# A layer of latent attention and gated MLP: one turn of three PSUM banks, later key stores, a float32 last block

## The chip, the core and the metric

The kernel runs on one core of a Trainium2 chip. The metric is the device time of one execution in microseconds (us), as a median of several runs. The core has five engines that work through queues of their own: TensorE (PE, matrix products; its loads of the stationary operand are listed as PEld), VectorE (DVE), ScalarE (ACT), GpSimd (POOL) and SyncE (SP), which here only issues transfers. PSUM, where matrix products arrive, has eight banks of 128 x 512 float32.

## What is computed

The layer takes `x`, 2048 tokens of 1024 features, projects it, mixes it in two branches, and projects back.

```python
y = rms_norm(h, norm_in_g)
proj = jnp.einsum("bsd,de->bse", y, w_in)
q_lat, kv_lat, k_rope, gate_mla, u, v, gate_gmlp = jnp.split(proj, bounds, axis=-1)
o_mla = mla_branch(q_lat, kv_lat, k_rope, q_norm_g, w_uq, kv_norm_g, w_ukv)
o_gmlp = gmlp_branch(jax.nn.gelu(u, approximate=False), jax.nn.gelu(v, approximate=False),
                     gmlp_ln_g, gmlp_ln_b, w_spatial, b_spatial)
o_mla = rms_norm(o_mla, out_norm_mla_g) * jax.nn.silu(gate_mla)
o_gmlp = rms_norm(o_gmlp, out_norm_gmlp_g) * jax.nn.silu(gate_gmlp)
h = h + jnp.einsum("bse,ed->bsd", jnp.concatenate([o_mla, o_gmlp], axis=-1), w_out)
return rms_norm(h, final_norm_g)
```

The attention branch has 8 heads of 64 + 32 (rotary) key features and 128 value features. The rotary key is one for all heads. The mask is causal by chunks of 64: a query sees all keys of its chunk and of the chunks before.

## The kernel before

Tokens are tiled by 512 (four tiles `t`), in two halves `hf` of two tiles. Nearly every product is made from three passes: each operand is split into a high part of a shorter float32 type (`fp32r`, names ending in `h`) and the rest (`l`), and high x high, low x high and high x low are added up in PSUM. Each half runs through the stages values of the gate (`v`), query latents, queries, key and value latents (`stage_kv`), keys and values (`stage_ukv`), gates (`gm`) and the gated MLP (`stage_ug`, products `u` and `g` with weights loaded as `ws_ug` and split into `wh_ug` on ScalarE and `wl_ug` on VectorE, and `sp`, a plain float32 product with the spatial matrix). `stage_kv` turns the rotary keys with a selecting matrix `sel` (L518), splits them on ScalarE and VectorE (L521, L82) and writes each part to `kh_d` or `kl_d` for all eight heads, 512 KB a store (L524). `stage_ukv` stores keys (L464) and values (`vh_d`, `vl_d`, L559, L560).

Attention runs over 32 units, 8 heads `h` by 4 query tiles `j` of 512 (heads 0 and 7 with `j` from 3 down). A unit has `nk` = 4j + 4 blocks of 128 keys, the last four of them on the diagonal. Block `kb` makes scores `ss` by three matmuls (L832 to L834), one exponential, the split into `ph` and `pl`, and three matmuls into `po` (L872 to L874). Odd blocks take their exponentials on ScalarE and their subtraction on VectorE (L82), even ones subtract on GpSimd (L866); row sums build up in `accv` and `accg` (L854, L870, L881). Diagonal block i uses columns from 128 i on, but at most from 256: the fourth (kb = nk - 1) has 256 columns, half of them filled with zero (L842, L843). Then the sums are turned and reduced (`pzs`, L92, L93), their reciprocals spread (`pzr`, L99), and the output scaled (L888).

Ahead of it, `row_maxima` makes a maximum for each query row: products `px` (L168), each read by one or two reductions into `mx` (L173, L175), and at the end of a unit `mz`, `pzm` (L145) and the last rows of `qh` (L146). Between the blocks stand products of the MLP's output projection (`pg`), handed out by `side()`, as long as there are any. After attention come the rows of the attention output: `mla_rows` (`sq`, `zm`, row sums `s`, the product `pr` with a column of ones, `zmh`, `zml`) and the projection `pm`.

PSUM during attention: `px` and `pzm` turn in two banks (`ps_x`), `pzs`, `pzr` and `pr` use one (`ps_z`), `ss` two, `po` one, `pe` two. A scheduler with a timeline of its own orders the instructions of each engine, so that small edits move others; each engine then works strictly in its order. The order excerpts below are from it.

## Time and profile before

| | |
|---|---|
| median of three timed runs | 1889.8 us (1889.35 to 1889.97) |
| profiled execution | 1891.02 us, of it the span 1889.2 |
| TensorE busy | 1857.7 us, 98% of the span |
| VectorE, ScalarE, GpSimd busy | 1111.1, 788.1, 582.8 us |
| granted clock of TensorE, mean | 0.994 |

Times in the rows are counted from the start of the span. Attention runs from about 1022 to 1702 us, the last projection from there to the end. Busy time says how long an engine had an instruction at hand; a printed matmul overlaps the next, so what a matmul costs is read from one start to the next. A granted clock of 1 is 2.4 GHz, 0.5 is 1.2.

### The profile page before, as it was taken

How to read it: one execution, taken by the hardware profiler on the slowest of the kernel's cores; microseconds unless marked ns; L12 is line 12 of the kernel's file. 1: busy time of each engine (PE TensorE's matmuls, PEld its weight loads, DVE VectorE, ACT ScalarE, POOL GpSimd, SP SyncE). 2: the span in 40 equal slices, each digit the busy share in tenths (PEclk: the TensorE clock that was granted, in tenths of full speed). 3: DMA queues.
4: the chain of work that ended last, by engine and by line, in shares of the span. 5: the costliest groups of instructions: out<-in, count | busy, mean ns of one | idle time of the engine just before them, and what ended most of it. 6: DMA issues, size and time to landing. Idle time of an engine off the chain costs nothing.

```text
span 1889.2 us, 24722 instructions
## 1 busy us (share of the span) xinstructions
PE 1857.7 (98%) x8638; PEld 1536.8 (81%) x8638; DVE 1111.1 (59%) x1866; ACT 788.1 (42%) x1440; POOL 582.8 (31%) x644
## 2 busy tenths in 40 slices
PE   8999999999999999999999999999999999999998
PEld 6888877888888887888887788888888888778886
DVE  7235454665622463557766677676677776665553
ACT  6232233522422332333213655555555555573332
POOL 5000100122100010012224645464545455564332
PEclk9999999999999999999998999999999999999999
DMA  7225387955432253986427653343425242445653
GB/s 253 91 74 190 104 249 255 306 158 156 156 105 73 97 195 90 290 273 190 135 91 226 181 156 101 106 125 110 142 68 166 76 132 83 141 162 182 201 190 107
DMA packets 251173, 292.28 MB, mean 155 GB/s; under 512 B 17188, under 2 KB 166692, under 8 KB 250792
## 3 DMA queue, kind: packets, MB, share of 16 engines
q1 hardware_dynamic: 250904, 290.69, 48.7%
q8 instruction: 69, 1.13, 0.3%
q14 instruction: 56, 0.46, 0.1%
q10 hardware_dynamic: 144, 0.00, 0.0%
HBM read 181.58 MB, written 111.15 MB: 155 GB/s over the span
## 4 chain that ended last, share of the span: by engine, by line
PE 90%; DMA 3%; DVE 3%; issue 2%; ACT 1%; POOL 1%; DVEq 0%; SPq 0%; POOLq 0%; ACTq 0%
PE px L168 3%; PE ss L832 3%; PE ss L833 3%; PE ss L834 3%; PE po L874 3%; PE po L872 3%; PE po L873 3%; PE pm L911 3%; PE pg L910 3%; PE pg L911 3%; PE pm L912 3%; PE pm L910 3%; PE u L107 3%; PE pg L912 3%; PE u L109 3%; PE g L109 3%
## 5 line engine op out<-in xcount | busy, mean ns | idle before, releaser
L175 DVE TENSOR_REDUCE mx<-px 128x1 f32<-128x512 f32 (+2 forms) x320 | 180.3, 580 | 34.0 <-PE px L168 31.6
L870 POOL TENSOR_TENSOR accg<-accg,p 128x512 f32<-128x512 f32 (+1 forms) x104 | 118.0, 1134 | 189.0 <-ACT p L864 138.4
L82 DVE TENSOR_TENSOR pl<-ss,ph 128x512 fp32r<-128x512 f32 (+2 forms) x160 | 93.2, 583 | 138.6 <-ACT ss L848 124.9
L866 POOL TENSOR_TENSOR pl<-p,ph 128x512 fp32r<-128x512 f32 (+1 forms) x128 | 150.9, 1179 | 40.2 <-ACT ph L865 19.3
L639 POOL TENSOR_TENSOR z<-gu,ggt 128x512 f32<-128x512 f32 x32 | 42.0, 1312 | 365.4 <-DVE ggt L627 245.0
L847 ACT ACTIVATE ph<-ss 128x512 fp32r<-128x512 f32 (+2 forms) x160 | 82.1, 513 | 130.7 <-PE ss L834 112.2
L874 PE MATMUL po<-pl,vh 128*128 128x512 f32 (+1 forms) x320 | 120.4, 376 | 5.3 <-POOL pl L866 3.7
L832 PE MATMUL ss<-qh,kh 100*128 100x512 f32 (+1 forms) x320 | 120.1, 375 | 1.4 <-ACT p L864 0.7
L872 PE MATMUL po<-ph,vh 128*128 128x512 f32 (+1 forms) x320 | 119.6, 374 | 0.2 <-ACT ph L847 0.2
L833 PE MATMUL ss<-ql,kh 96*128 96x512 f32 (+1 forms) x320 | 118.9, 372 | 0.0
L834 PE MATMUL ss<-qh,kl 96*128 96x512 f32 (+1 forms) x320 | 118.5, 370 | 0.0
L168 PE MATMUL px<-kh,qh 96*128 96x512 f32 (+2 forms) x320 | 111.2, 386 | 6.0 <-DVE mx L175 4.7
L873 PE MATMUL po<-ph,vl 128*128 128x512 f32 (+1 forms) x320 | 117.0, 365 | 0.0
L910 PE MATMUL pg<-woh,zgh 128*128 128x512 f32 x256 | 101.8, 398 | 0.0
L107 PE MATMUL u<-yh,wh_ug 128*128 128x512 f32 x256 | 101.7, 397 | 0.0
L911 PE MATMUL pm<-wol,zmh 128*128 128x512 f32 x256 | 101.6, 397 | 0.0
L107 PE MATMUL gm<-yh,wh_gm 128*128 128x512 f32 x256 | 101.0, 395 | 0.4 <-DVE kf L440 0.4
L911 PE MATMUL pg<-wol,zgh 128*128 128x512 f32 x256 | 101.3, 396 | 0.0
L912 PE MATMUL pg<-woh,zgl 128*128 128x512 f32 x256 | 100.7, 393 | 0.0
L108 PE MATMUL gm<-yl,wh_gm 128*128 128x512 f32 x256 | 100.4, 392 | 0.0
L910 PE MATMUL pm<-woh,zmh 128*128 128x512 f32 x256 | 100.4, 392 | 0.0
L109 PE MATMUL gm<-yh,wl_gm 128*128 128x512 f32 x256 | 100.4, 392 | 0.0
(567 smaller groups left out, 4938.1 us busy)
## 6 DMA issues: line engine op xcount, KB each, us to landing
ws_ug<-in_w_in SPq DMA_DIRECT2D x32, 512.0 KB, 5.0
xt<-in_x_t SPq DMA_DIRECT2D x16, 512.0 KB, 5.9
gv_d<-gv SPq DMA_DIRECT2D x32, 256.0 KB, 2.0
ws_gm<-in_w_in SPq DMA_DIRECT2D x16, 512.0 KB, 4.5
gt_d<-gth SPq DMA_DIRECT2D x32, 256.0 KB, 2.7
lgv<-gv_d SPq DMA_DIRECT2D x32, 256.0 KB, 3.5
wos<-in_w_out SPq DMA_DIRECT2D x16, 512.0 KB, 3.8
z_d<-z SPq DMA_DIRECT2D x32, 256.0 KB, 3.1
```

Of the source, the lines that this page charges most:

```text
L107: nc.tensor.matmul(ps, wh(d), xh(d), start=(d == 0), stop=False)
L109: nc.tensor.matmul(ps, wl(d), xh(d), start=False, stop=(d == n - 1))
L175: nc.vector.reduce_max(mx[:, b, c + 1 : c + 2], px[:, :w], axis=AX.X)
L832: nc.tensor.matmul(ss[:, l0:], kh[0:100, ks], qh[0:100, l0:], start=True, stop=False)
L833: nc.tensor.matmul(ss[:, l0:], kh[0:QH, ks], ql[0:QH, l0:], start=False, stop=False)
L834: last = nc.tensor.matmul(ss[:, l0:], kl[0:QH, ks], qh[0:QH, l0:], start=False, stop=True)
L872: nc.tensor.matmul(po[:, v0:], vh[:, vs, :], ph[:, v0:], start=(kb == 0), stop=False)
L873: nc.tensor.matmul(po[:, v0:], vl[:, vs, :], ph[:, v0:], start=False, stop=False)
L874: nc.tensor.matmul(po[:, v0:], vh[:, vs, :], pl[:, v0:], start=False, stop=(kb == nk - 1))
L910: nc.tensor.matmul(ps, h, ws[d][0][:, cs], start=(d == 0), stop=False)
L911: nc.tensor.matmul(ps, h, ws[d][1][:, cs], start=False, stop=False)
L912: nc.tensor.matmul(ps, lo, ws[d][0][:, cs], start=False, stop=(d == 7))
```

## The change

Three parts. (1) `ps_z` goes; `ps_x` has three banks, and `pzs`, `pzr` and `pr` take turns in it with `px` and `pzm`. (2) The two rotary products of a half add up in one PSUM tile, 32 rows each, are split by one copy and one subtraction, and wait in a tile of `xpool`; their four stores are held behind the last `vl_d` store of the half. (3) The last diagonal block is made from whole float32 operands, put together on GpSimd (`kf`, `qf`, `vf`), on its 128 columns: one score matmul, one exponential, one addition on VectorE, one output matmul.

```diff
--- before.py
+++ after.py
@@ -50,7 +50,7 @@
-    sel = cpool.tile([P, P], F32, name="sel")[:, 0:ROPE]
+    sel = cpool.tile([P, P], F32, name="sel")
@@ -512,20 +512,22 @@
                 r1s[t] = up.tile([P, 512], F32, tag="gu", name=f"kr1_{t}")
                 nc.vector.tensor_mul(r1s[t], ps, tab)
             lat = all_latents(ts, ys, ws, gkv, KR, "kv")
-            for t in ts:
-                tok = slice(t * 512, (t + 1) * 512)
-                ps2 = ps_t.tile([P, 512], F32, tag="pt", name=f"kr2{t}")
-                nc.tensor.matmul(ps2[0:ROPE, :], sel, r1s[t], start=True, stop=True)
-                h = lp.tile([P, 512], F32R, tag="oh", name=f"krh{t}")
-                lo = lp.tile([P, 512], F32R, tag="ol", name=f"krl{t}")
-                nc.scalar.copy(h[0:ROPE, :], ps2[0:ROPE, :])
-                sub_hi(lo[0:ROPE, :], ps2[0:ROPE, :], h[0:ROPE, :])
-                for dst, src in ((kh_d, h), (kl_d, lo)):
+
+            ps2 = ps_t.tile([P, 512], F32, tag="pt", name=f"kr2{hf}")
+            for k, t in enumerate(ts):
+                nc.tensor.matmul(ps2[0:64, :], sel[:, 32 - 32 * k : 96 - 32 * k], r1s[t], start=(k == 0), stop=(k == 1))
+            kr = xpool.tile([P, 2, 512], F32R, tag="xt", name=f"krs{hf}")
+            nc.scalar.copy(kr[0:64, 0, :], ps2[0:64, :])
+            sub_hi(kr[0:64, 1, :], ps2[0:64, :], kr[0:64, 0, :])
+            return lat, kr
+
+        def store_kr(ts, kr):
+            for k, t in enumerate(ts):
+                for i, dst in enumerate((kh_d, kl_d)):
                     nc.sync.dma_start(
-                        out=dst[NOPE:QH, :, tok],
-                        in_=src[0:ROPE, :].bitcast(F32).unsqueeze(1).broadcast_to([ROPE, H, 512]),
+                        out=dst[NOPE:QH, :, t * 512 : (t + 1) * 512],
+                        in_=kr[32 * k : 32 * k + 32, i, :].bitcast(F32).unsqueeze(1).broadcast_to([ROPE, H, 512]),
                     )
-            return lat
 
         def stage_ukv(hf, ts, lat, gates):
             w = weights(f"ukn_{hf}")
@@ -557,9 +559,10 @@
                         nc.scalar.activation(h, ps, AF.Copy, scale=rb)
                         nc.vector.scalar_tensor_tensor(lo, ps, rb, h.bitcast(F32), op0=ALU.mult, op1=ALU.subtract)
                         nc.sync.dma_start(out=vh_d[rows, cols], in_=h.bitcast(F32))
-                        nc.sync.dma_start(out=vl_d[rows, cols], in_=lo.bitcast(F32))
+                        stored = nc.sync.dma_start(out=vl_d[rows, cols], in_=lo.bitcast(F32))
                     if b % 2 == 0:
                         next(gates)
+            return stored
 
         def stage_gate(hf, ts, ys):
 
@@ -689,7 +692,8 @@
-            nc.sync.dma_start(out=sel, in_=a["sel"])
+            nc.gpsimd.memset(sel, 0.0)
+            nc.sync.dma_start(out=sel[:, 32:64], in_=a["sel"])
@@ -717,9 +721,10 @@
                     column_sums(mm_tile, zaccs[t], ssz[:, 4 * t : 4 * t + 4], f"zss{t}")
             next(gates)
             stage_uq(hf, ts, lat, gates)
-            lat = stage_kv(hf, ts, ys)
+            lat, kr = stage_kv(hf, ts, ys)
             next(gates)
-            stage_ukv(hf, ts, lat, gates)
+            with tc.issue_after(stage_ukv(hf, ts, lat, gates).ins):
+                store_kr(ts, kr)
             for _ in gates:
                 pass
             if hf == 1:
@@ -727,7 +732,7 @@
-                right_pool("ps_x", 2, space=PSUM)
+                right_pool("ps_x", 3, space=PSUM)
@@ -781,13 +786,12 @@
-        ps_z = pools["ps_z"] = pool("ps_z", 1, space=PSUM)
         def pz_tile(shape, nm):
-            return ps_z.tile(shape, F32, tag="pz", name=nm)
+            return pools["ps_x"].tile(shape, F32, tag="px", name=nm)
 
         def load_unit(h, j):
 
@@ -821,14 +825,39 @@
             qh, ql = qts[h, j], qls[h, j]
             po = ps_o.tile([P, 512], F32, tag="po", name=f"po{u}")
             nk = 4 * j + 4
+            end = slice(384, 512)
 
             for kb in range(nk):
                 i = kb - 4 * j
-                l0 = min(max(0, i) * P, 256)
+                if i == 0:
+
+                    kf = wk.tile([P, P], F32, tag="kf", name=f"kf{u}", bufs=1)
+                    qf = wk.tile([P, P], F32, tag="qf", name=f"qf{u}", bufs=1)
+                    vf = wk.tile([P, P], F32, tag="vf", name=f"vf{u}", bufs=1)
+                    for f, hi, lo in ((kf, khs[h, j], kls[h, j]), (qf, qh, ql)):
+                        nc.gpsimd.tensor_tensor(
+                            f[0:QH, :], hi[0:QH, end].bitcast(F32), lo[0:QH, end].bitcast(F32), op=ALU.add
+                        )
+                        nc.gpsimd.tensor_copy(f[96:100, :], hi[96:100, end].bitcast(F32))
+                    hi, lo = vts[h, j]
+                    nc.gpsimd.tensor_tensor(vf, hi[:, 3, :].bitcast(F32), lo[:, 3, :].bitcast(F32), op=ALU.add)
+                l0 = max(0, i) * P
                 kh, kl = khs[h, kb // 4], kls[h, kb // 4]
                 vh, vl = vts[h, kb // 4]
                 ks = slice((kb % 4) * P, (kb % 4 + 1) * P)
                 ss = ps_s.tile([P, 512], F32, tag="ss", name=f"ss{u}_{kb}")
+                if i == 3:
+                    last = nc.tensor.matmul(ss[:, end], kf[0:100, :], qf[0:100, :], start=True, stop=True)
+                    nc.scalar.copy(ss[64:128, 384:448], pools["neg"][64:128, :])
+                    p = ppool.tile([P, 512], F32, tag="p", name=f"p{u}_{kb}", bufs=3)
+                    nc.scalar.activation(p[:, end], ss[:, end], AF.Exp, scale=SCALE)
+                    acc = av if j > 0 else ag
+                    nc.vector.tensor_tensor(acc[:, end], p[:, end], acc[:, end], op=ALU.add)
+                    nc.tensor.matmul(po[:, end], vf, p[:, end], start=False, stop=True)
+                    next(maxima, None)
+                    with tc.issue_after(last.ins):
+                        side()
+                    continue
                 nc.tensor.matmul(ss[:, l0:], kh[0:100, ks], qh[0:100, l0:], start=True, stop=False)
                 nc.tensor.matmul(ss[:, l0:], kh[0:QH, ks], ql[0:QH, l0:], start=False, stop=False)
                 last = nc.tensor.matmul(ss[:, l0:], kl[0:QH, ks], qh[0:QH, l0:], start=False, stop=True)
@@ -838,10 +867,6 @@
                 if i >= 0:
 
                     nc.scalar.copy(ss[64:128, i * P : i * P + 64], pools["neg"][64:128, :])
-                if i == 3:
-                    nc.gpsimd.memset(ph[:, 256:384].bitcast(F32), 0.0)
-                    nc.gpsimd.memset(pl[:, 256:384].bitcast(F32), 0.0)
-                    l0 = 384
                 if kb in on_vector(u, nk):
 
                     nc.scalar.activation(ph[:, l0:], ss[:, l0:], AF.Exp, scale=SCALE)
@@ -871,7 +896,7 @@
                 vs = kb % 4
                 nc.tensor.matmul(po[:, v0:], vh[:, vs, :], ph[:, v0:], start=(kb == 0), stop=False)
                 nc.tensor.matmul(po[:, v0:], vl[:, vs, :], ph[:, v0:], start=False, stop=False)
-                nc.tensor.matmul(po[:, v0:], vh[:, vs, :], pl[:, v0:], start=False, stop=(kb == nk - 1))
+                nc.tensor.matmul(po[:, v0:], vh[:, vs, :], pl[:, v0:], start=False, stop=False)
                 next(maxima, None)
                 if kb == nk // 2 and u + 2 < len(units):
                     load_unit(*units[u + 2])
```

GpSimd at the boundary from unit 15 to 16 (the digits behind a name's letters are the unit, the block, and a running number), before:

```order
L870 TENSOR_TENSOR accg15_11385<-accg15_11385,p15_14_11647 128x256
L842 MEMSET ph15_15_11665 128x128
L866 TENSOR_TENSOR pl15_14_11645<-p15_14_11647,ph15_14_11644 128x256
L843 MEMSET pl15_15_11666 128x128
L132 MEMSET kh5_2_12054 4x512
L881 TENSOR_TENSOR accg15_11385<-accg15_11385,accv15_11366 128x512
L866 TENSOR_TENSOR pl16_0_11708<-accg16_11710,ph16_0_11707 128x512
```

and now:

```order
L895 TENSOR_TENSOR accg15_11356<-accg15_11356,p15_14_11626 128x256
L891 TENSOR_TENSOR pl15_14_11624<-p15_14_11626,ph15_14_11623 128x256
L838 TENSOR_TENSOR kf16_11673<-kh4_0_10502,kl4_0_11170 96x128
L841 COPY kf16_11673<-kh4_0_10502 4x128
L838 TENSOR_TENSOR qf16_11674<-qh4_0_10500,ql4_0_11168 96x128
L841 COPY qf16_11674<-qh4_0_10500 4x128
L906 TENSOR_TENSOR accg15_11356<-accg15_11356,accv15_11337 128x512
L843 TENSOR_TENSOR vf16_11675<-vh4_0_11172,vl4_0_11173 128x128
L891 TENSOR_TENSOR pl16_0_11686<-accg16_11688,ph16_0_11685 128x512
```

The two fills are gone; `kf`, `qf` and `vf` of the next unit stand between the last `pl` of a unit and the first of the next.

SyncE, directly behind the last `vl_d` store of the second half (`woh_d`, `wol_d`: split output weights; `kh`, `qh`: loads for the maxima), before:

```order
L321 DMA woh_d_82<-wos0_0h_6232 128x512
L322 DMA wol_d_83<-wos0_0l_6233 128x512
L321 DMA woh_d_82<-wos0_1h_6315 128x512
L131 DMA kh0_0_6596<-kh_d_76 96x512
L131 DMA kh0_1_6599<-kh_d_76 96x512
L131 DMA kh0_2_6602<-kh_d_76 96x512
L131 DMA kh0_3_6605<-kh_d_76 96x512
L126 DMA qh0_2_6608<-qh_d_74 96x512
L126 DMA qh0_1_7102<-qh_d_74 96x512
L126 DMA qh0_0_7504<-qh_d_74 96x512
L322 DMA wol_d_83<-wos0_1l_6316 128x512
L370 DMA ws_ug2_1_128_0_6327<-in_w_in 128x8x128
```

and now:

```order
L527 DMA kh_d_76<-krs1_5449 256x1x512
L527 DMA kl_d_77<-krs1_5449 256x1x512
L527 DMA kh_d_76<-krs1_5449 256x1x512
L527 DMA kl_d_77<-krs1_5449 256x1x512
L321 DMA woh_d_82<-wos0_0h_6221 128x512
L322 DMA wol_d_83<-wos0_0l_6222 128x512
L321 DMA woh_d_82<-wos0_1h_6304 128x512
L126 DMA qh0_2_6597<-qh_d_74 96x512
L126 DMA qh0_1_7091<-qh_d_74 96x512
L126 DMA qh0_0_7493<-qh_d_74 96x512
L322 DMA wol_d_83<-wos0_1l_6305 128x512
L370 DMA ws_ug2_1_128_0_6316<-in_w_in 128x8x128
```

The four stores have come in, and four `kh` loads have gone further back; `ws_ug2_1_128`, the weights of `g` for the second chunk, is the twelfth row of both.

TensorE at the end of the last unit, 31, before:

```order
L872 MATMUL po31_15312<-ph31_3_15360,vh7_0_14161 128x256
L873 MATMUL po31_15312<-ph31_3_15360,vl7_0_14162 128x256
L92 MATMUL pzs31t_15375<-ident_60,accg31_15320 128x128 x3
L874 MATMUL po31_15312<-pl31_3_15361,vh7_0_14161 128x256
L910 MATMUL pm12_0_15487<-woh0_15392,zmh12_0_15432 128x512
L911 MATMUL pm12_0_15487<-wol0_15393,zmh12_0_15432 128x512
L910 MATMUL pm12_1_15515<-woh0_15392,zmh12_0_15432 128x512
L911 MATMUL pm12_1_15515<-wol0_15393,zmh12_0_15432 128x512
L92 MATMUL pzs31t_15375<-ident_60,accg31_15320 128x128
```

and now:

```order
L92 MATMUL pzs31t_15329<-ident_60,accg31_15283 128x128 x2
L899 MATMUL po31_15267<-pl31_2_15309,vh7_0_14121 128x256
L856 MATMUL po31_15267<-p31_3_15322,vf31_15270 128x128
L92 MATMUL pzs31t_15329<-ident_60,accg31_15283 128x128 x2
L99 MATMUL pzr31b_15336<-ident_60,rs31_15328 128x128 x4
L935 MATMUL pm12_1_15469<-woh0_15346,zmh12_0_15386 128x512
L936 MATMUL pm12_1_15469<-wol0_15347,zmh12_0_15386 128x512
L1018 MATMUL pr12_15402<-ones_62,s1_12_15400 128x1
L937 MATMUL pm12_1_15469<-woh0_15346,zml12_0_15387 128x512
```

`pzr31b`, which before comes behind some twenty-five products `pm`, now follows `pzs31t` directly, and `pm12_1` comes first in place of `pm12_0`.

VectorE at the same place, before:

```order
L991 TENSOR_REDUCE s1_12_15446<-sq12_15425 128x128
L82 TENSOR_TENSOR pl31_3_15361<-ss31_3_15356,ph31_3_15360 128x128
L856 TENSOR_TENSOR accg31_15320<-ss31_3_15356,accg31_15320 128x128
L82 TENSOR_TENSOR zml12_0_15433<-zm12_0_15426,zmh12_0_15432 128x512
L93 TENSOR_REDUCE rs31_15374<-pzs31t_15375 128x4
L82 TENSOR_TENSOR zml12_1_15443<-zm12_1_15436,zmh12_1_15442 128x512
L886 RECIPROCAL rs31_15374<-rs31_15374 128x4
L82 TENSOR_TENSOR zml13_0_15463<-zm13_0_15456,zmh13_0_15462 128x512
L991 TENSOR_REDUCE s1_13_15476<-sq13_15455 128x128
L82 TENSOR_TENSOR zml13_1_15473<-zm13_1_15466,zmh13_1_15472 128x512
L888 TENSOR_TENSOR o31_15372<-pzr31b_15382,o31_15372 128x512
```

and now:

```order
L93 TENSOR_REDUCE rs31_15328<-pzs31t_15329 128x4
L911 RECIPROCAL rs31_15328<-rs31_15328 128x4
L1016 TENSOR_REDUCE s1_12_15400<-sq12_15379 128x128
L913 TENSOR_TENSOR o31_15326<-pzr31b_15336,o31_15326 128x512
L82 TENSOR_TENSOR zml12_0_15387<-zm12_0_15380,zmh12_0_15386 128x512
```

The row sum `s1_12` and the scaling of unit 31 now stand between the reciprocal and the first `zml`.

## Rows read from the trace of the kernel before

**Rows 1.** The page: busy time, share, instructions; then the chain by engine.

```profile
PE 1857.7 (98%) x8638; PEld 1536.8 (81%) x8638; DVE 1111.1 (59%) x1866; ACT 788.1 (42%) x1440; POOL 582.8 (31%) x644
...
PE 90%; DMA 3%; DVE 3%; issue 2%; ACT 1%; POOL 1%; DVEq 0%; SPq 0%; POOLq 0%; ACTq 0%
```

**Rows 2.** TensorE in order of time: start and length in us, line, operation.

```profile
1691.43 0.28 PE L832 MATMUL ss<-qh,kh 100*128 100x256 f32 x1
1691.55 0.28 PE L833 MATMUL ss<-ql,kh 96*128 96x256 f32 x1
1691.67 0.28 PE L834 MATMUL ss<-qh,kl 96*128 96x256 f32 x1
```

**Rows 3.** Chain of waits, two stretches: start and length in us, engine, tile.

```profile
861.66 0.89 PE sp L630 x8
...
1716.00 0.12 PE pr L993 x2
1716.12 0.34 PE pm L912
```

**Rows 4.** Waits of TensorE, 1400 to 1640 us: total us, times, longest.

```profile
PE px L168 <- DVE qh L146: 1.2, 2, 1.0
PE px L168 <- DVE mx L175: 1.1, 3, 0.5
```

**Rows 5.** Stretches: length, busy us of PE, PEld, DVE, ACT, POOL, clock, DMA.

```profile
1620.00:1627.00 7.00, 5.52 (x30) 4.16 (x29) 6.57 (x17) 1.99 (x6) 3.00 (x5) 1.00 0.61 196
1627.00:1630.50 3.50, 3.50 (x10) 2.73 (x9) 0.55 (x1) 1.25 (x3) 1.27 (x1) 0.51 0.00 0
```

**Rows 6.** Waits of TensorE, 240 to 290 us.

```profile
PE wspt L755 <- DVE wsp L746: 3.8, 1, 3.8
PE gm L107 <- DVE kf L440: 0.4, 1, 0.4
```

**Rows 7.** GpSimd by line and shape: count, busy us, mean ns, idle before.

```profile
L881 POOL TENSOR_TENSOR accg<-accg,accv 128x512 f32<-128x512 f32 x24 | 31.4, 1307 | 16.3 <-DVE accv L854 10.1 <-PE px L168 1.9 <-PE ss L834 1.7
...
L866 POOL TENSOR_TENSOR pl<-p,ph 128x256 fp32r<-128x256 f32 x32 | 24.8, 776 | 2.4 <-ACT ph L865 2.3
...
L842 POOL MEMSET ph<- 128x128 f32 x32 | 6.5, 204 | 0.0
```

**Rows 8.** In order of time, GpSimd, then TensorE, at a boundary of units.

```profile
1360.17 1.30 POOL L866 TENSOR_TENSOR pl<-accg,ph 128x512 fp32r<-128x512 f32 x1 [0.47 <-ACT ph L865]
...
1364.34 0.40 PE L874 MATMUL po<-pl,vh 128*128 128x512 f32 x1
```

**Rows 9.** Waits of TensorE, 1640 to 1712 us.

```profile
PE po L874 <- POOL pl L866: 2.2, 4, 0.9
PE po L874 <- DVE pl L82: 1.5, 1, 1.5
```

**Rows 10.** In order of time, GpSimd, then VectorE, the end of attention.

```profile
1691.99 0.74 POOL L866 TENSOR_TENSOR pl<-p,ph 128x256 fp32r<-128x256 f32 x1
...
1693.58 1.28 POOL L881 TENSOR_TENSOR accg<-accg,accv 128x512 f32<-128x512 f32 x1 [0.70 <-DVE accv L854]
...
1704.14 1.55 POOL L985 TENSOR_TENSOR zm<-zm,gm 128x512 f32<-128x512 f32 x1 [2.92 <-DMA gm<-gt_d]
...
1699.17 1.94 DVE L991 TENSOR_REDUCE s<-sq 128x128 f32<-128x1024 f32 x1
...
1703.27 0.69 DVE L93 TENSOR_REDUCE rs<-pzs31t 128x4 f32<-128x512 f32 x1 [1.17 <-PE pzs31t L92]
1703.88 0.68 DVE L82 TENSOR_TENSOR zml<-zm,zmh 128x512 fp32r<-128x512 f32 x1
```

**Rows 11.** Transfers in 40 slices, 748 to 764 us; ScalarE and TensorE in order.

```profile
GB/s 0 0 0 148 410 200 210 189 205 195 200 195 190 210 189 205 189 189 210 184 210 195 184 210 154 133 282 353 307 256 205 189 220 164 251 379 399 405 394 405
...
834.70 1.05 ACT L387 CAST wh_ug<-ws_ug 128x1024 fp32r<-128x1024 f32 x1 [4.42 <-DMA ws_ug<-in_w_in]
...
844.71 0.39 PE L109 MATMUL g<-yh,wl_ug 128*128 128x512 f32 x1
```

## The prediction

> **What bounds the kernel now.** I read the page's busy times and chain first, then the list of TensorE's waits, then single stretches of the trace. TensorE is busy for 1857.7 of 1889.2 us, and 90% of the chain that ends last is its work [rows 1]. So a matmul taken away in the middle of the program is worth its own time, and work on any other engine costs nothing until TensorE waits for it. The reader should look in the rows for two things only: what TensorE's steps cost from start to start (its printed durations overlap), and the few places where it waits.
>
> All sums are made for the profiled execution, 1891.0 us (span 1889.2 and 1.8 around it). It is 1.2 us above the median of the timed runs, 1889.8, and I take that off at the end.
>
> **The last diagonal block in float32.** Before, the fourth diagonal block of each of the 32 units has three score matmuls on 256 columns and three output matmuls on 256 columns. Such matmuls follow each other at 0.12 us from start to start [rows 2], so the block costs 6 x 0.12 = 0.72 us. Afterwards it is one score and one output matmul, float32, 128 columns. Two kinds of float32 matmul bound that price. Four of the `sp` matmuls (128 columns, two passes each, hence x8) take 0.89 us, 0.22 each. A lone `pr` matmul between matmuls of the other type takes 0.12 us and its successor 0.34 in place of 0.23, so 0.23 together, though it has one column [rows 3]. I take 0.23: the new ones are alone as `pr` is, and 128 columns cost no more in `sp`. A unit saves 0.72 - 0.46 = 0.26 us. I count 28 units, 28 x 0.26 = **-7.3 us**; the last four are paced by other engines and counted below. If a lone one cost 0.32, the saving would be 0.08 x 28 = 2.2 us.
>
> What the block gives to GpSimd: two adds on 96x128, two copies of 4x128 and one add on 128x128, and it loses two fills. No 128-column add is in the trace. From 512 columns to 256 an add falls from 1307 to 776 ns, a fill of 128x128 takes 204 [rows 7]; continuing the line gives about 0.5 us an add (an estimate), and a copy 0.2 to 0.25. That is 2.0 us a unit, less 0.4. In GpSimd's order these rows stand between the last `pl` of a unit and the first `pl` of the next, ahead of `accg<-accg,accv`. Before, at such a boundary, the first `pl` is done at 1360.17 + 1.30 = 1361.5 and TensorE uses it at 1364.34 [rows 8]: 2.9 us of cover. GpSimd stood idle for 0.47 us ahead of that `pl`, and for some time, 0.70 us in the row of another boundary [rows 10], ahead of `accg<-accg,accv`; the new work fills both. Some 1.3 us of cover should remain, and the matmuls that the new order puts between are fewer, so I charge +0.3 us for all boundaries up to the 28th; bounds 0 and +5.
>
> **The end of attention** has no output-projection matmuls left to fill in, and there TensorE already waits 2.2 us for `pl` of GpSimd and 1.5 for the last `pl` of VectorE [rows 9]. Take the boundary from unit 30 to 31, counting from the end of unit 30's last `pl`. Before, GpSimd starts `accg<-accg,accv` 0.85 us later, at 1693.58 against 1691.99 + 0.74 [rows 10]. Now 1.5 us of `kf`, `qf` come first, so `accg` ends at 2.8, `vf` at 3.3, the first `pl` at 4.6, where before it was about 3.5 (1693.58 + 1.28 + 1.30). TensorE waits for both, having only some 2 us of matmuls between. Behind that the order changes: `pzr31b` now stands directly behind `pzs31t`, with no projection matmul between, so TensorE waits out the column reduce (0.69 us [rows 10]) and the reciprocal; and `pr` and the first `zml` matmul stand early in the projection, while VectorE first does the 1.94 us row sum [rows 10], the product for unit 31 and then `zml`. By these durations TensorE is at the same point of the projection about 1.5 us later than before, although the 1.5 us wait for VectorE's `pl` goes with the block's subtraction. The two boundaries before it have less cover too; by the same count they lose 0.3 and 0.7 us. With a little for a spell at the lower clock, **+2.8 us**, bounds 0 and +6.
>
> **One ring of three banks.** Between 1400 and 1640 us TensorE waits for maxima: 1.2 us for `qh` and 1.1 us for `mx` [rows 4]. Maxima stand in bunches there, and two banks hold two. Around 1620 to 1627 TensorE is busy 5.52 of 7 us, and then follow 3.5 us at a granted clock of 0.51, the lower level of 1.2 GHz, which cost half of themselves, 1.7 us [rows 5]. A third bank can take 2.3 + 1.7 = 4.0 us at best. But VectorE is busy 6.57 of those 7 us, so a bank more lets TensorE run one reduce ahead, not empty the queue. Sums and spreads now take turns in the ring too; before they had a bank to themselves. I take half, **-2.0 us**, bounds +1 and -4. The run of maxima just before attention isn't counted: VectorE works there nearly without a gap, and its order hardly changes.
>
> **Rotary keys.** The two products cost TensorE the same, 4 passes a half. The stores leave the `oh`/`ol` slots, and the 0.4 us that TensorE waited for a late `kf` (L440, a tile of the keys' stage) [rows 6] may go, once in each half. The 3.8 us wait for `wsp` [rows 6] stays: the same loads stand ahead of it in SyncE's queue. **-0.8 us**, bounds 0 and -5, the wait for `wsp` and a spell at the lower clock behind it.
>
> In the second half the stores now stand, on SyncE, behind the last `vl_d` store and ahead of `woh_d`, the `qh` loads, the second `ws_ug` and `lgv`. From 750 to 757 us, where the old ones ran, the transfers came to 184 to 210 GB/s [rows 11], the slices there being 0.4 us long, so 512 KB take about 2.6 us and four 10.5. Four `kh` loads of 192 KB, at the 300 GB/s that the same row reaches 2.6 us, move behind `ws_ug`. It landed at 834.70, when its cast starts [rows 11]; now at about 834.7 + 10.5 - 2.6 = 842.6 (at 160 GB/s, near the row's low end, 845). The cast takes 1.05 us [rows 11] and the low part on VectorE, at twice a subtraction of 512 columns [rows 10], 1.3 more; TensorE wants the low part for `g` at 844.71 [rows 11]. It comes at 844.9 to 847.3. All of this shifts together if the stage comes earlier. **+1.5 us**, bounds 0 and +5 (with a spell at half clock). In the first half nothing behind the stores is needed so soon.
>
> **Sum.** -7.3 + 0.3 + 2.8 - 2.0 - 0.8 + 1.5 = -5.5. 1891.0 - 5.5 = 1885.5 for a profiled execution, less 1.2: **1884** in a timed run.
>
> **Rivals.**
> (a) Everything meets its cover: no late `ws_ug`, a ring that clears the bunches and the spell of low clock, an end that loses 1 us: -7.3 - 4.0 - 0.8 + 1.0 = -11.1, **1879**. For it: the bunches are short, and 0.2 us decides over `ws_ug`. Against it: VectorE is nearly full in the bunches.
> (b) The moved stores arrive late: `ws_ug` at 845 and a spell of low clock after the stall, and the end costs its bound: -7.3 - 1 - 0.4 + 4 + 5 = +0.3, **1890**. For it: the queue is full there. Against it: it needs two bounds at once.
> (c) Slower: GpSimd becomes the pace at every boundary. Its five new operations are estimated at 2.0 us; the cover left is 1.3 us, so from about 3.3 us on TensorE waits for each first `pl`. At 4.0 us, twice my estimate, 0.7 us at 27 boundaries are 19 us, against -5.5: about **1903**. For it: no row shows operations so small on parts of tiles. Against it: the line from 512 to 256 columns.
> (d) The adds block each other. Beside VectorE's `zml` (1703.88, both inputs in SBUF) GpSimd's `zm` took 1.55 us [rows 10]; an add of that size takes 1307 ns [rows 7], so 0.25 were lost. The new sum of the last block reads `p` from SBUF, where the old one read the scores from PSUM, so such a loss can now come at each boundary. It is covered except at the last three, where a lost GpSimd operation of up to 1.3 us may stand ahead of the add: 3 x 0.7 = 2 us, **1886**. The Trainium skill, SBUF — State Buffer, section "Who interferes with whom", states the rule: a VectorE instruction with two SBUF inputs and a GpSimd instruction that reads SBUF lock each other out, whichever starts first. The `zm` row agrees with it in kind.
>
> **Chances.** Forecast (1880 to 1888) 0.52, (a) 0.20, (b) 0.14, (c) 0.06, (d) 0.08. About 0.2%, 3.8 us, is what a measurement of this kernel can tell: faster means below 1886.0. The forecast lies below that in three cases of four (0.39), (a) wholly (0.20), (d) in a part (0.03): faster 0.62. (c) and a quarter of (b) end above 1893.6: slower 0.09. The rest, 0.29, is no change. Leaving out (c) and the far half of (b), and the far end of (a), the range is 1876 to 1892.
>
> **What would show it.** The block: the score and output matmuls of 128 columns at 0.22 to 0.23 us each and six fewer of 256 columns per unit; at 0.3 the first term falls. GpSimd: the adds near 0.5 us, and TensorE's wait for `pl` not above 5 us in all; at 15 us (c) holds. Ring: TensorE's waits for `mx` and `qh` between 1400 and 1640 at half, and no stretch at 0.51 near 1627. Stores: `ws_ug`'s cast starting near 843, and a wait of `g` for `wl_ug` of 0 to 3 us. End: waits before `pzr31b`, `pr` and the first `zml` matmul.

## The result, and the profile after

The changed kernel is slower. Its median is 1910.7 us (1907.2 to 1914.5) against 1889.8 us (1888.8 to 1890.1); the ratio is 1.0112, 95% interval 1.0098 to 1.0127. The profiled execution took 1910.7 us with a span of 1908.9. The forecast was 1884 with a range of 1876 to 1892, so both its sign and its range were wrong.

The page after, busy times and chain, answers to [rows 1]:

```profile
PE 1857.1 (97%) x8574; PEld 1530.4 (80%) x8574; DVE 1114.8 (58%) x1832; ACT 781.4 (41%) x1406; POOL 653.8 (34%) x741
...
PE 91%; DVE 4%; POOL 1%; issue 1%; ACT 1%; DMA 1%; SPq 0%; POOLq 0%; DVEq 0%; ACTq 0%
```

TensorE is busy as long as before, in a span 19.7 us longer. Where the time is lost is seen when the span is divided at four events: the first product of the rotary keys' stage, the first score matmul (attention begins), the first column sum of unit 28, and the end. Each number is the difference of two first starts (the last one ends with the span), in us:

```
kernel   start   keys' stage to    first score    sum of unit 28
                 first score       to unit 28     to the end
before   198.6   823.0             642.3          225.3
after    196.6   813.8             634.6          263.9
```

The first stretch gained 9.2 us, where the prediction's terms for it, -0.8 and +1.5, come to a small loss. The second gained 7.7, somewhat less than the 9.0 of its terms (-7.3, +0.3 and -2.0). The last one lost 38.6. The waits of TensorE after, from 1683 us to the end (total us, times, longest):

```profile
PE pr L1018 <- DVE s L1016: 22.2, 15, 1.5
PE pm L935 <- ACT zmh L1013: 1.5, 2, 1.1
PE pm L937 <- DVE zml L82: 0.8, 1, 0.8
```

The first line stands nowhere in the lists of before: the one-column product `pr`, which sums the squares of a block of 128 tokens, waits for the row sum `s`, 15 times. The stretch in windows (length, busy us of PE, PEld, DVE, ACT, POOL, granted clock, DMA, GB/s), first the whole projection, then one wait and what follows it:

```profile
1683.40:1908.90 225.50, 193.48 (x800) 152.21 (x800) 107.94 (x114) 58.15 (x125) 85.67 (x111) 0.94 0.44 141
1744.00:1747.10 3.10, 1.57 (x8) 0.91 (x7) 3.10 (x4) 0.75 (x2) 1.69 (x1) 1.00 0.78 257
1747.10:1750.50 3.40, 3.40 (x10) 2.62 (x9) 1.22 (x3) 0.72 (x2) 1.11 (x2) 0.51 0.79 227
1774.50:1777.90 3.40, 3.40 (x9) 2.62 (x10) 1.48 (x4) 0.72 (x2) 1.11 (x2) 0.51 0.75 213
```

Five of the fifteen waits, the first of them at 1746, are followed by 3.4 us at a granted clock of 0.51 or 0.50, the lower level of 1.2 GHz; two of the five are shown. A sixth such spell, at 1685.7, stands among the first waits of the projection.

**The loop that paces the end.** These are the rows of one block in the kernel after (start and length in us, engine, line, operation, idle time before), VectorE, then GpSimd, then TensorE:

```profile
1739.43 0.75 DVE L940 SCALAR_TENSOR_TENSOR h<-pm,rm,h 128x512 f32<-128x512 f32 x1 [4.12 <-PE pm L937]
1742.26 2.30 DVE L1047 SCALAR_TENSOR_TENSOR h<-h,fs,gfin 128x1024 f32<-128x1024 f32 x1 [2.07 <-POOL fs L1043]
1744.48 1.92 DVE L1016 TENSOR_REDUCE s<-sq 128x128 f32<-128x1024 f32 x1
...
1742.19 3.51 POOL L1010 TENSOR_TENSOR zm<-zm,gm 128x512 f32<-128x512 f32 x2
...
1744.53 0.40 PE L936 MATMUL pm<-wol,zmh 128*128 128x512 f32 x1
1746.45 0.38 PE L1018 MATMUL pr<-ones,s 128*128 128x1 f32 x2 [1.53 <-DVE s L1016]
1746.70 0.48 PE L935 MATMUL pm<-woh,zmh 128*128 128x512 f32 x1
```

`pm`'s first half (`pm..._0`) takes its bank from the same ring of three as `pr`, and in program order `pr` of block n+1 is allocated ahead of `pm_0` of block n (the kernel prepares a block's rows one block early). So `pr` of the next block goes directly ahead of `pm_0` of this one: TensorE's order is two products of `pm14_1`, then `pr14`, the 24 of `pm13_0`, the other 22 of `pm14_1`, two of `pm15_1`, `pr15`, and so on. (Before, `pr` stands behind thirteen of the products of a `pm_0`.) That closes a circle. `pm_0` ends, VectorE adds it to `h`, ScalarE squares it, GpSimd makes the factor `fs`, VectorE scales (L1047), and behind that in its queue does the row sum `s` of a later block, for which `pr` waits, ahead of the next `pm_0`. From the end of `pm_0` at 1739.4 to `pr` at 1746.45 it takes 7.0 us. TensorE has 24 other matmuls to fill them with, 24 x 0.227 = 5.4 us, and waits out the rest. From `pr` to `pr` a block takes 13.03 us after, 14.61 where a spell at the lower clock follows, against 11.13 us before, where `pr` has a bank that no `pm` needs.

### The profile page after: what moved, and what is told of

It is laid out like the page before. It is cut to its first block, busy times and chain, and to the rows that moved or that the text cites. A ratio compares the mean times of both kernels' runs of the same rounds, so it can differ in the third digit from the quotient of the medians.

```text
span 1908.9 us, 24481 instructions
## 1 busy us (share of the span) xinstructions
PE 1857.1 (97%) x8574; PEld 1530.4 (80%) x8574; DVE 1114.8 (58%) x1832; ACT 781.4 (41%) x1406; POOL 653.8 (34%) x741
## 4 chain that ended last, share of the span: by engine, by line
PE 91%; DVE 4%; POOL 1%; issue 1%; ACT 1%; DMA 1%; SPq 0%; POOLq 0%; DVEq 0%; ACTq 0%
PE px L168 3%; PE ss L861 3%; PE po L897 3%; PE ss L862 3%; PE po L899 3%; PE pg L936 3%; PE pg L935 3%; PE po L898 3%; PE ss L863 3%; PE gm L107 3%; PE u L107 3%; PE u L109 3%; PE pg L937 3%; PE gm L109 3%; PE u L108 3%; PE g L109 3%
## 5 line engine op out<-in xcount | busy, mean ns | idle before, releaser
L82 DVE TENSOR_TENSOR pl<-ss,ph 128x512 fp32r<-128x512 f32 (+1 forms) x128 | 84.0, 656 | 110.5 <-ACT ss L873 107.3
L872 ACT ACTIVATE ph<-ss 128x512 fp32r<-128x512 f32 (+1 forms) x128 | 73.2, 572 | 123.4 <-PE ss L863 111.4
L861 PE MATMUL ss<-qh,kh 100*128 100x512 f32 (+2 forms) x288 | 112.8, 392 | 1.3 <-ACT accg L889 0.7
L899 PE MATMUL po<-pl,vh 128*128 128x512 f32 (+2 forms) x288 | 110.9, 385 | 2.4 <-POOL pl L891 2.4
L897 PE MATMUL po<-ph,vh 128*128 128x512 f32 (+2 forms) x288 | 109.8, 381 | 3.1 <-ACT o L908 2.5
L862 PE MATMUL ss<-ql,kh 96*128 96x512 f32 (+2 forms) x288 | 109.8, 381 | 0.0
L168 PE MATMUL px<-kh,qh 96*128 96x512 f32 (+2 forms) x320 | 104.9, 391 | 4.5 <-DVE mx L175 2.8
L863 PE MATMUL ss<-qh,kl 96*128 96x512 f32 (+2 forms) x288 | 109.2, 379 | 0.0
L898 PE MATMUL po<-ph,vl 128*128 128x512 f32 (+2 forms) x288 | 108.6, 377 | 0.0
L937 PE MATMUL pm<-woh,zml 128*128 128x512 f32 x256 | 101.3, 405 | 0.8 <-DVE zml L82 0.8
```

The source lines that it names most:

```text
L861: nc.tensor.matmul(ss[:, l0:], kh[0:100, ks], qh[0:100, l0:], start=True, stop=False)
L862: nc.tensor.matmul(ss[:, l0:], kh[0:QH, ks], ql[0:QH, l0:], start=False, stop=False)
L863: last = nc.tensor.matmul(ss[:, l0:], kl[0:QH, ks], qh[0:QH, l0:], start=False, stop=True)
L897: nc.tensor.matmul(po[:, v0:], vh[:, vs, :], ph[:, v0:], start=(kb == 0), stop=False)
L898: nc.tensor.matmul(po[:, v0:], vl[:, vs, :], ph[:, v0:], start=False, stop=False)
L899: nc.tensor.matmul(po[:, v0:], vh[:, vs, :], pl[:, v0:], start=False, stop=False)
```

## Experiments

**The pairing of `pr` and `pm_0`.** Theory A: the two sharing one ring is the cause. Three kernels: `pr` moved out of the ring, `pm_0` moved out of it, and the ring alone on the kernel before.

```
 e1, on the kernel after:
-            pr = pz_tile([P, 512], f"pr{b}")
+            pr = ps_o.tile([P, 512], F32, tag="po", name=f"pr{b}")
 e2, on the kernel after:
-            steps = project([px_tile, pe_tile], ws, zh, zl, ...)
+            steps = project([lambda s, n: ps_s.tile(s, F32, tag="ss", name=n), pe_tile], ws, zh, zl, ...)
 e3, on the kernel before: only right_pool("ps_x", 3), no ps_z, pz_tile from ps_x
```

> The changed kernel, but the small product pr of each row block takes the bank of po, which is idle after attention, in place of a turn in the ring of three. Theory A (in one ring pr of the next block has to come ahead of pm_0 of this block, so TensorE waits 15 times about 1.5 us for a row sum, and loses clock behind it): the waits of pr for s fall from 22.2 us to under 4, the stretches at half clock after 1710 us go, and the time is 1910.7 - 22 - 5 x 1.7 - 2, about 1875 us. Theory B (the projection is slow for another cause, such as the transfers or GpSimd's new load): pr waits stay or move, and the time stays above 1900.

> The changed kernel, but pm_0, not pr, leaves the ring: it takes the two banks of the scores. Theory A says that it is the pairing of the two in one ring, not the place of pr, so this gives the same as moving pr: about 1875 us, within 2 us of it. If it is pr's tile alone that is served late (a slot that comes free late), this one keeps the waits, and stays near 1905.

> The kernel before with the one ring of three banks and nothing else. Theory A: the projection loses its 30 to 38 us here too, the maxima win 0 to 4, so 1917 to 1928 us. If the loss needs the float32 block or the moved stores as well, it stays within 5 us of 1890.

Measured: `e1` 1873.9 us (ratio to before 0.9914, 0.9899 to 0.9929), `e2` 1872.1 (0.9907, 0.9890 to 0.9923), `e3` 1925.0 (1.0186, 1.0171 to 1.0201). Either half of the pair moved away makes the kernel 37 to 39 us faster than the kernel after, and the ring alone, without the other two changes, makes the kernel before 35 us slower. All three came out as theory A expected (`e2` 1.8 us from `e1`). The order of `e1` and `e2` is the same on every engine, and in both `pr` stands again behind thirteen products of a `pm_0`. The waits of `e1` in its last stage, 1685 us to the end:

```profile
PE pm L937 <- DVE zml L82: 0.8, 1, 0.8
PE pr L1018 <- DVE s L1016: 0.4, 1, 0.4
PE pm L935 <- ACT zmh L1013: 0.3, 1, 0.3
```

And one block of `e1`, VectorE, GpSimd, TensorE:

```profile
1740.09 2.03 DVE L1016 TENSOR_REDUCE s<-sq 128x128 f32<-128x1024 f32 x1 [1.88 <-ACT sq L1009]
...
1745.52 1.28 DVE L1047 SCALAR_TENSOR_TENSOR h<-h,fs,gfin 128x1024 f32<-128x1024 f32 x1 [1.27 <-POOL fs L1043]
...
1739.62 2.55 POOL L1010 TENSOR_TENSOR zm<-zm,gm 128x512 f32<-128x512 f32 x2 [0.33 <-ACT sq L1009]
...
1745.64 0.28 PE L1018 MATMUL pr<-ones,s 128*128 128x1 f32 x2
```

The row sum ends at 1742.1 and `pr` runs at 1745.64, 3.5 us later, without a wait. From `pr` to `pr` it is 11.13 us again, and no spell at the lower clock is left in that stage but the last, at the end of the program. Theory A stands.

**The scaling that doubles.** In the rows after, L1047 takes 2.30 us; in `e1` the same instruction takes 1.28. After, it starts 0.07 us behind GpSimd's two `zm` products, which take 3.51 us in place of 2.55. By a rule of the Trainium skill, SBUF — State Buffer, "Who interferes with whom", a VectorE instruction with two SBUF inputs and a GpSimd instruction that reads SBUF exclude each other, and one with at most one SBUF input (outside the two-port modes) doesn't contend. To test that, `e9` gives L1047 its weights from PSUM, in the two score banks that are idle by then, and scales in two halves of 512 columns; TensorE's and GpSimd's instructions stand in the same order as in the kernel after.

```
+        gps = [ps_s.tile([P, 512], F32, tag="ss", name=f"gps{c}") for c in range(2)]
+        for c in range(2):
+            nc.scalar.copy(gps[c], gfin[:, 512 * c : 512 * c + 512])
...
-                    xt[:, cs], xt[:, cs], ss[:, 2:3], gfin[:, cs], op0=ALU.mult, op1=ALU.mult
+                    xt[:, cs], xt[:, cs], ss[:, 2:3], gps[c // 512], op0=ALU.mult, op1=ALU.mult
```

> The kernel after, with the last norm's weights copied once into the two score banks (free by then), so that VectorE's final scaling L1047 reads one input from SBUF and one from PSUM, in two halves of 512 columns; the order of TensorE's and GpSimd's work is the same, row for row. Theory: in the kernel after the scaling takes 2.24 us in place of 1.29 only because GpSimd's zm products (both inputs in SBUF, 1.77 us in place of 1.30) run at the same moment and the two engines hold each other up. Then each half takes 0.75 us beside GpSimd, zm is back near 1.3 us, the row sum s comes some 0.8 us sooner in each block, the wait of pr falls from 1.5 to about 0.7 us in each of 15 blocks (from 22 us to about 11), and some of the spells at the lower clock go: 1893 to 1900. Rival: the scaling is long for another cause (the row it stands in, the late wake-up by GpSimd), the halves take over 1.0 us each, pr waits as long as before: 1909 to 1913.

Measured: 1894.3 us (1892.0 to 1895.9; ratio to before 1.0031, 1.0020 to 1.0043), 16.4 us less than the kernel after. The same place in `e9`, GpSimd and VectorE:

```profile
1741.10 2.54 POOL L1013 TENSOR_TENSOR zm<-zm,gm 128x512 f32<-128x512 f32 x2
...
1741.17 1.41 DVE L1049 SCALAR_TENSOR_TENSOR h<-h,fs,gps 128x512 f32<-128x512 f32 x2 [2.07 <-POOL fs L1046]
1742.49 1.98 DVE L1019 TENSOR_REDUCE s<-sq 128x128 f32<-128x1024 f32 x1
```

and the wait of `pr` in the list of TensorE's waits:

```profile
PE pr L1021 <- DVE s L1019: 10.4, 15, 0.8
```

The two still start 0.07 us apart, and neither is longer than alone (a half takes 0.744 us in the mean, and the two halves of the last block 0.748 each in `e1`). The wait of `pr` fell from 22.2 to 10.4 us, a block from 13.03 (or 14.61) to 12.17 us, and the five spells at the lower clock are gone. So of the 36.8 us between the kernel after and `e1`, some 16 came from two engines blocking each other at that one place, spells included (the medians are of two sets of runs, in which the kernel before stood 1.8 us apart). In the traces it is 20.1 of 37.8 us: from the sum of unit 28 to the end the kernel after takes 263.9 us, `e9` 243.8 and `e1` 226.1. The rest is the circle itself. The trace agrees with the rule in both of its halves, and gives it a size: 1.0 us on a scaling of 1.3.

**The three changes taken apart.** `e4` is the kernel before with the float32 block alone, `e5` with the keys alone, `e8` with both; `e8` is the kernel after without its ring.

```
 e8, on the kernel after:
-                right_pool("ps_x", 3, space=PSUM)
+                right_pool("ps_x", 2, space=PSUM)
+        ps_z = pools["ps_z"] = pool("ps_z", 1, space=PSUM)
-            return pools["ps_x"].tile(shape, F32, tag="px", name=nm)
+            return ps_z.tile(shape, F32, tag="pz", name=nm)
```

> The kernel before with the float32 last block and nothing else. By the prediction's first term 0.26 us a unit on 28 units and a loss at the end of attention: 1884 to 1887 us. If the block brings its price in full in all 32 units, 1881. If GpSimd's new operations hold TensorE at the boundaries of units, above 1890.

> The kernel before with the change to the rotary keys alone (one product for two blocks, stores behind the values' stores). Theory, from the trace after: the four old stores of 512 KB held up SyncE's queue from 248.7 to 256.8 us, ahead of everything that it issues later in that half; without them the load of wsp is issued some 6 us sooner in its stage, TensorE's 3.8 us wait for wsp and the 3.4 us at a granted clock of 0.5 behind it both go, and the stage u starts at about 313 in place of 321.2 us. Time 1880 to 1884, no wait of TensorE for wsp in the list. Rival, as the prediction had it: the wait for wsp stays, since the load's place in the queue is the same, and only 0.8 us go: 1888 to 1890. A second rival: the stores are only moved, and TensorE waits for ws_ug in the second half (+1.5 or more, with a spell at the lower clock +4): 1884 to 1887.

> The kernel after without the ring: float32 block and rotary keys, but two banks for maxima and one for sums and spreads as before. Theory: the float32 block alone moved nothing (1888.5 against 1890.1), because TensorE met the maxima sooner and waited 6.1 us for them in two banks; the ring of three is what lets the block's saving through. Then this kernel has the gain of the keys alone, some 8 us: 1879 to 1883, attention (first score to first pm) some 680 us long, waits for mx above 4 us. It is 7 us slower than the kernel after with pr in a bank of its own (1873.9). Rival: the parts add up, each with its own gain, and the ring is worth the 2.2 us that attention gained when it was added alone: 1875 to 1877, attention 675 us.

Measured: `e4` 1888.5 us (0.9993, 0.9983 to 1.0002: no difference, which none of its three expectations had), `e5` 1885.0 (0.9978, 0.9969 to 0.9987), `e8` 1879.6 (0.9961, 0.9948 to 0.9974). The expectation of `e5` was met in the trace (no wait for `wsp`) and missed in the time by 1 us; that of `e8` was met in the time and missed in the length of attention, 675 us in place of 680. The same stretches as above show the parts more sharply than the times do, since the start of the keys' stage alone varies by 3.2 us. Each row is one profiled execution, and about 1 us lies between `before` and `e4` in the first stretch, where the float32 block has no part:

```
kernel (parts)           start  keys' stage to  first    first score  unit 28
                                first maximum   score    to unit 28   to end
before                   198.6  675.5           147.5    642.3        225.3
e3 ring                  197.2  675.2           146.3    640.7        263.6
e4 float32               196.7  676.4           147.5    642.1        226.1
e5 keys                  199.9  667.5           149.3    642.0        225.5
e8 keys, float32         198.3  667.5           149.9    636.0        226.0
e1 all, pr elsewhere     198.3  667.5           146.2    634.7        226.1
e2 all, pm_0 elsewhere   196.8  667.5           146.2    631.1        228.4
```

(The third column runs from the first maximum product to the first score.) The keys save 8.0 us up to the first maximum. With two banks 1.8 to 2.4 of these are lost in the run of maxima before attention; with the ring nothing is. Up to unit 28 the float32 block seems to save 6.0 us (`e5` to `e8`, and `e3` to `e1`), but 0.2 in `e4`. `e4` and `e8` have the same order of matmuls in attention, row for row; the windows of `e4` (columns as above) show the difference:

```profile
1052.45:1055.87 3.42, 3.42 (x10) 2.64 (x9) 3.12 (x6) 2.30 (x5) 1.63 (x2) 0.50 1.15 215
1410.85:1414.27 3.42, 3.42 (x11) 2.64 (x10) 0.26 (x2) 2.19 (x4) 1.27 (x1) 0.50 0.00 0
1499.60:1503.00 3.40, 3.40 (x8) 2.69 (x9) 1.63 (x5) 1.21 (x2) 0.57 (x2) 0.50 0.44 152
1625.90:1629.30 3.40, 3.40 (x10) 2.62 (x9) 1.11 (x4) 1.42 (x3) 1.28 (x1) 0.50 0.00 0
```

`e4` has four spells at the lower level inside attention. In `e8` the granted clock from the first of them on is full to the end of attention:

```profile
1019.40:1691.10 671.70, 658.43 (x3178) 543.40 (x3177) 461.66 (x893) 386.93 (x800) 412.54 (x471) 1.00 0.42 131
```

Matched matmul by matmul, `e4` falls behind `e8` by 1.5 to 1.6 us at each of the four and keeps its distance between them, 6.1 in all: that is the 6 us. The spells in `e4` come behind short stalls, the longest of 1.15 us; but `e8` has the same stalls at the same matmuls, in the lists of waits to within 0.1 us each, and no spell behind them. What decides over that stays open. It also means that the expectation of `e8` had the wrong reason: the missing gain of `e4` was not due to waits for maxima in two banks, since TensorE waits 2.4 us for `mx` in attention in both kernels.

The other rows have spells too, and with them apart the parts look different. `before` and `e5` have one of 3.4 us in that stretch (rows 5 show it at 1627), worth some 1.5 by the four of `e4`; `e3`, `e8` and `e2` have none; `e1` and the kernel after have one of 6.8 us. It comes behind a wait of 1.7 us for a load of maxima keys, which `e2`, with the same order, has as well. The wait is the same line in both lists; the windows are those of the kernel after, then of `e2`:

```profile
PE px L168 <- DMA kh<-kh_d: 1.7, 1, 1.7
1576.40:1583.30 6.90, 6.21 (x20) 4.74 (x19) 4.23 (x9) 3.41 (x6) 3.80 (x3) 0.51 0.10 38
1575.40:1582.30 6.90, 6.16 (x30) 4.90 (x31) 5.15 (x11) 4.43 (x8) 3.83 (x3) 1.00 0.20 69
```

So up to unit 28, without spells, it is about 640.8 us before and 640.7 with the ring alone (`e3`): nothing. With the float32 block alone it is 636.0 (`e8`; `e4` is that and its spells): -4.8. With both it is 631.1 (`e2`): -9.7, of which up to 0.9 lie in a spell at the start of attention that all have and that is shorter in `e2`. The two are worth more together than added up, so the theory that `e8` was made for, that the ring lets the block's saving through, is right in part. How it does so wasn't followed further.

**The end of attention.** `e10` is `e1` with the old block in units 28 to 31. One line of the edit:

```
-                if i == 3:
+                if i == 3 and u < 28:
                     last = nc.tensor.matmul(ss[:, end], kf[0:100, :], qf[0:100, :], start=True, stop=True)
```

> The kernel after with pr in the output bank (1873.9 when run before), and the float32 block only in units 0 to 27; the last four units have the old block again. It prices the end of attention, for which the prediction charged +2.8 us. From the traces: from the sum of unit 28 to the end it took 225.3 us before, 226.1 with the float32 block there. Theory: the float32 block gains nothing in the last four units, since VectorE and GpSimd pace them: 0.5 to 1 us less, 1872 to 1874. By the prediction's count it would be 2.8 us less, 1871. Rival: the block saves 0.26 us a unit there too, and this kernel is 1 us slower, 1875.

Measured: 1870.5 us (1869.6 to 1874.6; ratio to before 0.9911, 0.9897 to 0.9924). Beside the 0.9914 of `e1` that decides nothing. In the traces the stretch from the sum of unit 28 to the end is 223.3 us against 226.1: 2.8 us less, as the prediction's count had it, and not the 0.5 to 1 of the expectation's own theory. `e1`, `e2` and `e10` are the fastest kernels of this study, 0.9% below the kernel before and 1.9 to 2.1% below the kernel after; which of the three is best the timed runs don't tell.

## Why the prediction was wrong, point by point

**One ring of three banks** is the step that failed. It named sums and spreads as the ring's new users and bounded the term by +1 and -4, from stretches of attention alone [rows 4, 5]. The ring has two more users, `pr`, which the change itself names, and `pm_0`, which stood in the ring of two before, and they come in the last stage, 188 us that the step never looked at. The order now in force was there to be read in the scheduler's order: `pr` directly ahead of each `pm_0`, `s` directly behind the scaling. Of the +38.6, 22.2 us are waits of `pr` for `s`; spells follow five of them. The part on the end of attention saw one such `pr` (that of block 12) and charged the wait once, where it comes in fifteen blocks. So a case of +38.6 us had no place among the rivals. In attention itself the number came out near the -2.0 by luck: 642.3 to 640.7 us when the ring was added alone (-1.6), 636.0 to 634.7 with the other parts (-1.3). The waits for `mx` and `qh` between 1400 and 1640 did go, all 2.3 us of them, but in `e3` a wait of 1.8 us for `kh` came in their place, and its -1.6 is the spell at 1627 that it lacks. The -1.3 has the 6.8 us spell of `e1` in it; in `e2`, which has none, it is -4.9.

**Rotary keys** came out much better than -0.8. The prediction kept the 3.8 us wait for `wsp`, since "the same loads stand ahead of it in SyncE's queue". The loads do, but four stores of 512 KB (L524) stood there as well, and it moved them in its own text without taking them off this queue. SyncE in the kernel before (start, length of the issue), from the third of the four on:

```profile
250.20 1.88 SPq L524 DMA_DIRECT2D kh_d<-krh  x1
252.17 2.39 SPq L464 DMA_DIRECT2D kh_d<-kn_0h  x1
254.65 2.04 SPq L524 DMA_DIRECT2D kl_d<-krl  x1
...
281.39 0.41 SPq L743 DMA_DIRECT2D wsp<-in_w_spatial  x1
```

The first two of the four took 0.59 and 0.56 us; then every issue up to 260.6, the keys' stores L464 among them, takes 1.6 to 2.4, where L464 in the kernel after takes 0.3 to 0.4 at this place. The queue is held up. (The kernel after shows the same behind the stores' new place: 0.60, 0.63, 1.94 and 2.45 us, and the next two loads 2.46 and 2.26.) After, `wsp` is issued at 273.66; counted from the start of the keys' stage that is 77.1 us in place of 82.8, so 5.7 us sooner. The wait is gone, and so is the spell at 0.5 behind it, 3.8 + 1.7 of the 8.0 us; `e5`, with the keys alone, has neither of them. Of the other 2.5, three short waits of the kernel before that are gone as well make 0.9: the 0.4 for `kf` that the prediction named, and 0.3 and 0.2 for parts of the values. The rest wasn't followed further.

**The late `ws_ug`** was right in its working and fell on the free side. After, ScalarE's cast, VectorE's low part and the matmul that needs it:

```profile
832.36 1.05 ACT L387 CAST wh_ug<-ws_ug 128x1024 fp32r<-128x1024 f32 x1 [8.30 <-DMA ws_ug<-in_w_in]
...
833.44 1.23 DVE L82 TENSOR_TENSOR wl_ug<-ws_ug,wh_ug 128x1024 fp32r<-128x1024 f32 x1 [10.05 <-ACT wh_ug L387]
...
834.75 0.39 PE L109 MATMUL g<-yh,wl_ug 128*128 128x512 f32 x1
```

Counted from the matmul, the cast starts 2.4 us ahead in place of 10.0 [rows 11]: 7.6 us later, where 7.9 was forecast. The low part is done 0.08 us before TensorE wants it. No wait; the forecast was +1.5, with bounds that held 0.

**The float32 block** held in its price, and its saving depends on the ring. The price of 0.23 us was right: at a place in the kernel after an output matmul and its successor stand like this,

```profile
1357.07 0.39 PE L856 MATMUL po<-p,vf 128*128 128x128 f32 x2
1357.21 0.48 PE L861 MATMUL ss<-qh,kh 100*128 100x512 f32 x1
1357.53 0.39 PE L862 MATMUL ss<-ql,kh 96*128 96x512 f32 x1
```

so 0.14 until the successor, and the successor 0.32 in place of 0.23: 0.23 together. With the boundaries the forecast was -7.0 up to unit 28. The -6.0 of two pairs of kernels has different spells in it; without spells it is -4.8 beside two banks for the maxima and -9.6 beside the ring (`e3` to `e2`). With the ring's own term the two were to save 9.0, and saved 9.7. GpSimd's new operations, by line and shape (busy us, mean ns, idle before):

```profile
L838 POOL TENSOR_TENSOR qf<-qh,ql 96x128 f32<-96x128 f32 x32 | 15.1, 472 | 2.4
L843 POOL TENSOR_TENSOR vf<-vh,vl 128x128 f32<-128x128 f32 x32 | 14.8, 463 | 2.8 <-issue 1.2 <-DMA vl<-vl_d 0.9 <-PE po L856 0.6
...
L841 POOL COPY qf<-qh 4x128 f32<-4x128 f32 x32 | 10.3, 321 | 1.8
```

Adds of 0.47 us where 0.5 was estimated, copies of 0.3 where 0.2 to 0.25 was; TensorE's wait for `pl` in attention is 2.4 us. Rival (c) falls. Rival (d) was right in kind: the add of the last block on VectorE (L855, two inputs in SBUF) takes from 0.28 us to 0.60 beside GpSimd's work in 31 of the units, and in the last one, beside a `zm` product:

```profile
1679.53 1.34 DVE L855 TENSOR_TENSOR accg<-p,accg 128x128 f32<-128x128 f32 x1 [0.85 <-POOL accg L895]
1679.44 1.28 POOL L1010 TENSOR_TENSOR zm<-zm,gm 128x512 f32<-128x512 f32 x1
```

TensorE waits 0.4 us for that add, and for none of the others by its list: 0.4 us, where (d) had 2. No experiment took this add apart; what blocking was shown to cost, it cost at the last scaling.

**The end of attention**, +2.8, held: `e10` has it at 2.8 when the block is taken back there. Against the kernel before, the stretch from unit 28 on is only 0.8 longer in `e1` (225.3 to 226.1), but the kernel before has a spell of 3.4 us in it, at 1702.1, that `e1` and `e10` lack. Its waits came where they were named, 1.2 us before `pzr31b`, 0.85 before the first `pr` and 0.8 before the first `zml` matmul.

Without the pair in one ring the parts come to 1889.2 - 1872.8 = 16.4 us of gain in `e1`, where the prediction summed to 5.5. That it would then have missed on the other side is mostly the keys' doing (8.0 for 0.8), then the end's (0.8 for 2.8, the spell), the late `ws_ug` that was not late (1.5), and the ring's, which takes 1.3 off the run of maxima before attention (147.5 to 146.2).

## What to carry to other kernels

When buffers are merged into one ring, list every user of the ring in every stage, not only in the stage for which the merge is meant, and for each user write down who is allocated directly ahead of it and what that one waits for. If the one ahead waits for something that hangs on the one behind, a round ago, the ring has closed a loop, and the turn of that loop against TensorE's work in it is the price, times the rounds. And when a load is late, look at everything that is queued ahead of it, stores as well: a queue that is held up shows as a run of long issues.

## What the runs showed of the hardware

VectorE's scaling of 128x1024 with both inputs in SBUF took 2.24 us in the mean beside GpSimd's products, the last 28 of which took 1.77 each; apart they took 1.29 and 1.30, and with one of VectorE's inputs in PSUM the two ran at the same time at 1.41 (two halves) and 1.29 us.

The same attention matmuls in the same order, with the same stalls to within 0.1 us each, ran in one profiled execution with four spells of 3.4 us at the lower clock level and in another with none (`e4`, `e8`); `e1` and `e2`, with one order on every engine, ran with a spell of 6.8 us and without it. The four alone cost 1.5 to 1.6 us each, 6.1 together, more than any single term of the forecast but the float32 block's. A gain of a few microseconds in such a kernel is better read from the lengths of its stretches, spells counted apart, than from two times.
